# A fourth pair of split-weight buffers for two of the working tiles, and splits up to three chunks ahead

## The chip, the cores and the metric

The kernel runs on one NeuronCore of a Trainium2 chip. The metric is the device time of one execution in microseconds (us); several executions are timed and the median is given. A profile is one further execution, recorded by the hardware profiler.

## What is computed

Two layers of a hybrid diffusion backbone over 256 latent tokens and 256 context tokens, model width 1024, all in 32-bit floats:

```python
for l in range(DEPTH):                                  # DEPTH = 2
    # sh, sc, g: nine vectors per stream from the conditioning: s_c @ w_mod[l] + b_mod[l]
    x = x + 0.5 * g1 * swiglu(modulate(rms_norm(x, norm_g[l, 0]), sh1, sc1), ffn_w_in[l, 0], ffn_w_out[l, 0])
    h = h + 0.5 * cg1 * swiglu(...)                     # the context stream, same weights
    y, yc = token_mixer(modulate(rms_norm(x, ...)), modulate(rms_norm(h, ...)), ...)
    x = x + g2 * y
    x = x + 0.5 * g3 * swiglu(...)                      # second FFN; h too, in layer 0 only
```

`swiglu` has D_FF = 2816. The token mixer projects with one wide `w_in`, runs gated linear attention (4 heads), neighbourhood attention (16 heads) and grouped-query attention (8 heads), multiplies each result by a branch matrix, gates and adds them, and multiplies by `w_out`. The weights are read once from HBM, about 343 MB of traffic in all.

## The kernel before, in words

**Weights as a stream of chunks.** Every weight matrix is cut into chunks of 128 partitions x 1024 floats (512 KB), and `Program.chunk` (L281) puts them into one list in the order of use. A product in full precision is made of three matmuls (`mm3`, L494): weight and activation are each split into a part that TensorE's fast fp32r format holds exactly (`hi`) and the rest (`lo`), and hi·hi, hi·lo and lo·hi are added up in PSUM. So each chunk passes three places: a DMA on SyncE's queue (SP) loads it into a `w_raw` tile (L369), ScalarE (ACT) copies it, rounded, into `w_hi` (L382), and GpSimd (POOL) subtracts into `w_lo` (L385). TensorE (PE) then reads `w_hi` and `w_lo`.

**Buffers.** There are RAW_BUFS = 3 raw tiles and SPLIT_BUFS = 3 pairs of `w_hi` and `w_lo`. All other working tiles of the kernel (activations, attention weights, `mod_w` loads, temporaries of the norms) come from one pool `slot` of SLOTS = 54 tiles of 128 x 512 floats (`S`, L454).

**When a chunk is split.** The generator `splitter` (L373) runs through the chunks; its condition and the bookkeeping in `Program.run` (L355) are:

```python
for j, (src, a, b, do, halves) in enumerate(specs):
    while j > state["ci"] + SPLIT_AHEAD or (j >= SPLIT_BUFS and j - SPLIT_BUFS not in ended):
        yield None
    load(j + 1)
    ...
    load(j + 1 + RAW_BUFS)
...
fn(parts.pop(ci))
if ci + 1 not in self.kept:
    ended[ci] = self.clock.now
if ci in self.kept:
    ended[ci - 1] = self.clock.now
```

Here `ci` is the chunk whose matmuls are being issued. Chunk j is split once chunk j - SPLIT_BUFS has ended, and at most SPLIT_AHEAD chunks ahead. After the split of chunk j, chunk j + 3 is loaded into the raw tile that chunk j leaves.

**Pairs.** Most chunks are used one by one. Some are used two at a time: the first is kept (`kept`) and its matmuls are interleaved with those of the second, and neither has ended before both have. Two such pairs follow each other at the start of each FFN (`up` with `both`, L899: four chunks c0 to c3 for the two halves of the first block of the up-projection) and in `proj_f2` (L1085: queries and keys of the gated linear attention, twice per layer). The norm ahead of them delivers its result `u` tile by tile (`norm_chain`, L788; `need`, L831), in two halves r of 256 tokens, and the pairs let PE work on the first half while VectorE (DVE) makes the second. The last down-projection of an FFN and of `merge_out` (L1881) also end on a pair, so that the norm can start on one half.

**Order.** All instructions are issued in one order, decided while the program is built. A model clock (`Clock`, L54) estimates when each instruction would run; chunks are the main line, and at every `tick` (L351) a round is made: first the splitter, then pending norms and evacuations, then side jobs (attention heads, the conditioning vectors `mods`), each of which issues its next instruction once the model says that its inputs are there (`Gated`, L174). The model knows when the split buffers come free; it has no entry for the tiles of `slot`. Each engine then takes its own instructions strictly in this order, and waits on semaphores for the data and for the tiles it overwrites.

Of the kernel before, what the change touches and what calls it, by code (L numbers as in the profile page):

```python
# [36 lines left out]
C_GATE = 7712  # L37

RAW_BUFS = 3
SPLIT_BUFS = 3  # L40
SPLIT_AHEAD = 2
SLOTS = 54
LANES = 2
PE_MARGIN = 0.5
OTHER_SLACK = 0.1
# [155 lines left out]
class Program:  # L201
# [153 lines left out]
    def run(self):  # L355
# [17 lines left out]
        def splitter():  # L373
# [4 lines that stand above are left out]
                hi = self.wpool.tile([P, a, b], F32, name="w_hi", tag="w", padded_shape=[P, 1024 // b, b])  # L378
                lo = self.wpool.tile([P, a, b], F32, name="w_lo", tag="w", padded_shape=[P, 1024 // b, b])
                self.clock.floor[hi.name] = self.clock.floor[lo.name] = ended.get(j - SPLIT_BUFS, 0.0)  # L380
                raw = raws[j]
# [51 lines left out]
def tile_backbone(ctx: ExitStack, tc: tile.TileContext, I: dict, out: bass.AP):  # L433
# [4 lines left out]
    sml = ctx.enter_context(tc.tile_pool(name="sml", bufs=4))  # L438
    slot = ctx.enter_context(tc.tile_pool(name="slot", bufs=SLOTS))
    upool = ctx.enter_context(tc.tile_pool(name="upool", bufs=16))  # L440
    rpool = ctx.enter_context(tc.tile_pool(name="rpool", bufs=RAW_BUFS))
    wpool = ctx.enter_context(tc.tile_pool(name="wpool", bufs=2 * SPLIT_BUFS))
    psa = ctx.enter_context(tc.tile_pool(name="psa", bufs=4, space=PS))
# [1627 lines left out]
```

## Time and profile before

| | |
|---|---|
| median of 3 runs | 2881.67 us (2880.91 to 2881.89) |
| profiled execution | 2878.06 us |
| its span, first to last instruction | 2876.3 us |
| PE busy | 2777.6 us, 97% of the span |
| DVE, ACT, POOL busy | 58%, 35%, 45% of the span |
| DMA | 120 GB/s over the span |
| granted TensorE clock, mean | 0.985 |

The profile says for each engine how long it was busy. An idle stretch ends when the last thing that the engine waited for arrives, and the profile names that instruction ("idle before, <- releaser"). Time on the engine with hardly any idle stretches (PE here) is what the span consists of; its idle stretches and the stretches at the lower clock are what can be won. PEld is TensorE's loading of weights into the array, which overlaps the matmuls. POOL's times are rough. L196 and L169 are the helpers that issue all instructions, so instructions are told apart by the names of their tiles.

### The profile page before, as it was taken

Reading aid. Unit: us, or ns where it says so; the run is one execution under the profiler, and the core shown is the slowest. Engines: PE = TensorE matmul, PEld = TensorE weight load, DVE = VectorE, ACT = ScalarE, POOL = GpSimd, SP = SyncE. Lnnn points to the kernel's source line nnn. Section 1 sums busy time; section 2 is a strip of 40 time slices with the busy share of each in tenths; the row PEclk is TensorE's granted clock in tenths of the full one; section 3 lists DMA queues with packets and bytes.
Section 4 is the critical chain, followed back from the end, with each engine's and each line's share of the span. In section 5 each row is a group of like instructions: output and inputs, shape, how many; then the busy total and the mean of one; then the engine's idle time right before and its main releaser. Section 6 shows DMA issues by size and latency. Waiting matters only on the chain.

```text
span 2876.3 us, 39661 instructions
## 1 busy us (share of the span) xinstructions
PE 2777.6 (97%) x15547; PEld 2330.8 (81%) x15547; DVE 1662.6 (58%) x2970; ACT 1007.2 (35%) x1598; POOL 1288.1 (45%) x585
## 2 busy tenths in 40 slices
PE   8999998999999999999999989999999998999999
PEld 6888877778777888877888878888787777899899
DVE  5654566768765675675545575212555659757522
ACT  2222223433444344322312212222244345454443
POOL 3444433224333442434444434444433455657687
PEclk9999999999999999999999989999999999999999
DMA  6444443224222222433444434333323334435554
GB/s 228 159 147 133 151 129 107 77 81 131 80 73 78 81 74 62 161 125 109 144 143 139 161 102 146 101 96 99 110 70 85 95 100 115 132 103 180 172 184 155
DMA packets 295647, 346.46 MB, mean 120 GB/s; under 512 B 15541, under 2 KB 238806, under 8 KB 295460
## 3 DMA queue, kind: packets, MB, share of 16 engines
q1 hardware_dynamic: 294964, 343.58, 38.0%
q8 instruction: 122, 2.00, 0.3%
q14 instruction: 65, 0.53, 0.1%
q0 software_dynamic: 320, 0.28, 0.0%
q10 hardware_dynamic: 176, 0.07, 0.0%
HBM read 342.83 MB, written 1.05 MB: 120 GB/s over the span
## 4 chain that ended last, share of the span: by engine, by line
PE 86%; DVE 8%; issue 4%; POOL 1%; DMA 0%; ACT 0%; SPq 0%; DVEq 0%; POOLq 0%; ACTq 0%
PE up L169 28%; PE pf L169 17%; PE dn L169 15%; PE pt L169 15%; PE a_s L196 2%; PE a_t L196 2%; PE n_o L196 1%; POOL w_lo L196 1%; PE g_o L196 1%; PE q_o L196 1%; PE g_U L196 1%; PE a_qk L196 1%; DVE rs_a L196 1%; DVE z L169 1%; DVE a_p L196 1%
## 5 line engine op out<-in xcount | busy, mean ns | idle before, releaser
L196 POOL TENSOR_TENSOR w_lo<-w_raw,w_hi 128x1024 fp32r<-128x1024 f32 (+1 forms) x508 | 1228.2, 2422 | 1538.3 <-ACT w_hi L196 1480.3
L196 ACT CAST w_hi<-w_raw 128x1024 fp32r<-128x1024 f32 (+1 forms) x504 | 520.6, 1036 | 993.5 <-issue 311.9
L169 PE MATMUL up<-u_hi,w_lo 128*128 128x512 f32 (+1 forms) x1504 | 534.3, 355 | 16.1 <-POOL w_lo L196 16.0
L169 PE MATMUL up<-u_hi,w_hi 128*128 128x512 f32 (+1 forms) x1504 | 536.5, 357 | 6.4 <-DVE u_hi L196 4.1
L169 PE MATMUL up<-u_lo,w_hi 128*128 128x512 f32 (+1 forms) x1504 | 534.3, 355 | 5.0 <-DVE u_lo L196 4.8
L196 DVE SCALAR_TENSOR_TENSOR mod_acc<-mod_w,scv,mod_acc 128x512 f32<-128x512 f32 x364 | 372.7, 1070 | 57.3 <-DMA mod_w<-w_mod 57.0
L169 PE MATMUL dn<-ff_h,w_hi 128*128 128x512 f32 (+1 forms) x1528 | 396.8, 349 | 0.0
L169 PEld LDWEIGHTS up<-u_hi,w_hi 128*128 128x128 f32 x1504 | 290.9, 193 | 56.0 <-issue 11.0
L169 PEld LDWEIGHTS up<-u_hi,w_lo 128*128 128x128 f32 x1504 | 290.9, 193 | 54.9 <-POOL w_lo L196 17.1
L169 PEld LDWEIGHTS up<-u_lo,w_hi 128*128 128x128 f32 x1504 | 290.7, 193 | 43.4 <-DVE u_lo L196 6.0
L169 PEld LDWEIGHTS dn<-ff_h,w_hi 128*128 128x128 f32 x1528 | 267.6, 189 | 38.9 <-ACT w_hi L196 1.7
L169 PE MATMUL dn<-ff_h,w_lo 128*128 128x512 f32 (+1 forms) x764 | 265.9, 348 | 0.0
L169 PE MATMUL pt<-w_hi,u_hi 128*128 128x512 f32 x640 | 261.8, 409 | 0.0
L169 PE MATMUL pf<-u_hi,w_hi 128*128 128x256 f32 (+1 forms) x736 | 250.9, 341 | 10.3 <-DVE u_hi L196 7.0
L169 PE MATMUL pt<-w_hi,u_lo 128*128 128x512 f32 x640 | 250.8, 392 | 0.0
L169 PE MATMUL pt<-w_lo,u_hi 128*128 128x512 f32 x640 | 250.5, 391 | 0.0
L169 PE MATMUL pf<-u_hi,w_lo 128*128 128x256 f32 (+1 forms) x736 | 239.9, 326 | 8.7 <-POOL w_lo L196 8.7
L169 PE MATMUL pf<-u_lo,w_hi 128*128 128x256 f32 (+1 forms) x736 | 240.3, 327 | 5.8 <-DVE u_lo L196 5.7
L169 DVE TENSOR_TENSOR ff_h<-ff_a,up 128x512 f32<-128x512 f32 (+1 forms) x88 | 53.3, 620 | 317.0 <-PE up L169 278.7
L169 PE MATMUL pf<-y,w_hi 128*128 128x512 f32 (+1 forms) x768 | 195.6, 345 | 3.1 <-DVE y L196 1.9
L169 PEld LDWEIGHTS pf<-u_hi,w_hi 128*128 128x128 f32 x736 | 143.7, 195 | 30.9 <-issue 9.4
L169 DVE SCALAR_TENSOR_TENSOR x<-dn,ff_g,x 128x256 f32<-128x256 f32 x112 | 47.1, 478 | 202.0 <-PE dn L169 201.8
(227 smaller groups left out, 4043.0 us busy)
## 6 DMA issues: line engine op xcount, KB each, us to landing
w_raw<-ffn_w_in SPq DMA_DIRECT2D x176, 512.0 KB
w_raw<-w_in SPq DMA_DIRECT2D x168, 512.0 KB
mod_w<-w_mod SPq DMA_DIRECT2D x288, 256.0 KB
w_raw<-ffn_w_out SPq DMA_DIRECT2D x80, 512.0 KB
w_raw<-w_branch SPq DMA_DIRECT2D x48, 512.0 KB
w_raw<-w_out SPq DMA_DIRECT2D x16, 512.0 KB
w_raw<-ffn_w_out SPq DMA_DIRECT2D x16, 256.0 KB
n_rel<-nat_rpb SPq DMA_DIRECT2D x32, 109.5 KB
```

Source lines behind the costliest of these rows:

```text
L169: return real(*args, **kw)
L196: return real(*args, **kw)
```

## The change

```diff
 RAW_BUFS = 3
-SPLIT_BUFS = 3
-SPLIT_AHEAD = 2
-SLOTS = 54
+SPLIT_BUFS = 4
+SPLIT_AHEAD = 3
+SLOTS = 52
```

There are now four pairs `w_hi`, `w_lo`; chunk j is split once chunk j - 4 has ended, and up to three chunks ahead of the one in use. Two of the 54 working tiles go. Nothing else in the text differs; the order of instructions is worked out anew by the same rules.

## Rows read from the trace of the kernel before

**Rows 1.** The page: busy time of each engine and its share of the span.
```profile
PE 2777.6 (97%) x15547; PEld 2330.8 (81%) x15547; DVE 1662.6 (58%) x2970; ACT 1007.2 (35%) x1598; POOL 1288.1 (45%) x585
```

**Rows 2.** The waits of PE, whole span: for whom, us in total, times, longest.
```profile
PE up L169 <- POOL w_lo L196: 16.0, 4, 6.8
PE pf L169 <- POOL w_lo L196: 8.7, 3, 4.8
```

**Rows 3.** Timeline of PE, where it waits for a split: start, us, [idle before].
```profile
47.52 0.39 PE L169 MATMUL up<-u_hi,w_lo 128*128 128x256 f32 x1 [1.13 <-POOL w_lo L196]
...
438.59 0.58 PE L169 MATMUL pf<-u_hi,w_lo 128*128 128x256 f32 x1 [4.81 <-POOL w_lo L196]
...
497.10 0.39 PE L169 MATMUL pf<-u_hi,w_hi 128*128 128x256 f32 x1 [0.51 <-ACT w_hi L196]
499.54 0.39 PE L169 MATMUL pf<-u_hi,w_lo 128*128 128x256 f32 x1 [1.93 <-POOL w_lo L196]
...
1307.54 0.58 PE L169 MATMUL up<-u_hi,w_lo 128*128 128x256 f32 x1 [6.76 <-POOL w_lo L196]
...
1702.33 0.58 PE L169 MATMUL up<-u_hi,w_lo 128*128 128x256 f32 x1 [6.30 <-POOL w_lo L196]
...
2135.63 0.39 PE L169 MATMUL pf<-u_hi,w_hi 128*128 128x256 f32 x1 [1.02 <-ACT w_hi L196]
2138.12 0.39 PE L169 MATMUL pf<-u_hi,w_lo 128*128 128x256 f32 x1 [1.99 <-POOL w_lo L196]
...
2686.10 0.39 PE L169 MATMUL up<-u_hi,w_lo 128*128 128x256 f32 x1 [1.82 <-POOL w_lo L196]
```

**Rows 4.** Timelines of ACT and POOL where the second pair's split begins.
```profile
1299.06 2.00 ACT L196 CAST w_hi<-w_raw 128x1024 fp32r<-128x1024 f32 x2 [24.18 <-PE up L169]
...
1300.19 9.62 POOL L196 TENSOR_TENSOR w_lo<-w_raw,w_hi 128x1024 fp32r<-128x1024 f32 x2 [22.41 <-ACT w_hi L196]
```

**Rows 5.** Stretches after a stall (first: before one): us, busy by engine, PEclk, DMA.
```profile
430.00:433.50 3.50, 3.50 (x31) 3.50 (x30) 3.50 (x12) 1.44 (x2) 0.31 (x1) 1.00 0.00 0
...
438.59:443.00 4.41, 4.41 (x20) 4.41 (x21) 0.00 (x0) 0.00 (x0) 2.28 (x1) 0.50 0.64 153
...
1307.54:1313.50 5.96, 5.96 (x28) 5.96 (x29) 0.00 (x0) 0.00 (x0) 2.27 (x1) 0.50 0.73 224
...
1702.33:1706.10 3.77, 3.77 (x18) 3.77 (x19) 0.00 (x0) 0.00 (x0) 2.27 (x1) 0.51 0.51 155
...
499.50:504.00 4.50, 4.46 (x26) 4.47 (x27) 4.47 (x8) 0.46 (x1) 2.32 (x1) 0.68 0.61 150
2138.00:2143.00 5.00, 4.88 (x28) 4.88 (x29) 4.96 (x10) 0.00 (x0) 2.40 (x2) 0.66 0.64 175
```

**Rows 6.** Timeline of SP: loads of `w_raw`, the fourth chunk of two sites among them.
```profile
395.65 0.37 SPq L369 DMA_DIRECT2D w_raw<-w_in  x1
...
1261.30 0.38 SPq L369 DMA_DIRECT2D w_raw<-ffn_w_in  x1
```

**Rows 7.** Timeline of DVE: the last `u` tiles at two sites.
```profile
435.06 1.28 DVE L196 SCALAR_TENSOR_TENSOR u_lo<-n_t,mod,u_hi 128x256 fp32r<-128x256 f32 x3
...
1300.57 1.27 DVE L196 SCALAR_TENSOR_TENSOR u_lo<-n_t,mod,u_hi 128x256 fp32r<-128x256 f32 x3
```

**Rows 8.** Instructions on `w_lo` (ns, min/median/max), and ACT's waits for `w_hi`.
```profile
L196 POOL TENSOR_TENSOR w_lo<-w_raw,w_hi x508: 1258/2396/7294, 20.1 to 2865.7; 128x1024 fp32r<-128x1024 f32 x158, 128x512 fp32r<-128x512 f32 x12
...
ACT w_hi L196 <- PE up L169: 246.2, 63, 24.2
```

**Rows 9.** Timelines of POOL and DVE in the norm before the first pair.
```profile
406.89 5.14 POOL L196 TENSOR_TENSOR w_lo<-w_raw,w_hi 128x1024 fp32r<-128x1024 f32 x2 [11.26 <-ACT w_hi L196]
...
409.76 0.15 DVE L196 TENSOR_SCALAR rs_v<-n_ss 128x2 f32<-128x2 f32 x1
409.94 2.12 DVE L196 TENSOR_SCALAR rs_s<-rs_v 128x2 int32<-128x2 int32 x1
```

**Rows 10.** Groups of instructions, 930 to 1160 us: the last step of layer 0's grouped-query heads.
```profile
L196 ACT CAST y<-q_o 128x512 fp32r<-128x512 f32 x8 | 4.7, 586 | 15.3 <-PE q_o L196 15.3
```

## The prediction

> **What bounds the kernel now.** I read the page first. PE is busy for 2777.6 us, 97% of the span of 2876.3 us, so all that can be won on other engines lies in the 98.7 us in which PE is idle, and in stretches at the lower clock [rows 1]. POOL is busy for under half of the span, so splitting is not a rate limit; if it costs anything, it does so at single places. The waits of PE say so: waits for `w_lo` make 24.7 us, in only seven waits [rows 2]. Third, the timeline of PE, looked up for these waits: they lie at 47, 439, 500, 1308, 1702, 2138 and 2686 us, and two are preceded by a shorter wait for the `w_hi` of the same chunk [rows 3]. Each of the seven is the same place in the code: two pairs of chunks follow each other, and the second chunk of the second pair, c3, is missing. There are eight such places; at the eighth, in layer 1, PE waits for `u` instead. With three buffers c0, c1 and c2 fill them all, and c3 can be split only when PE has read c0 to the end, which in a pair is the end of the pair. The ACT row at 1299.06 shows it: ACT sits idle for 24.18 us and is released by the matmul of `up`, and only then are c3 and c4 split, 2.00 us on ACT and 9.62 us on POOL [rows 4]. PE has run through what c2 alone allows by 1300.8 and stands until 1307.54.
>
> Fourth, the stretches behind these waits. Just before a stall the granted clock is 1.00; behind the three long ones it is 0.50 for 4.4 to 6.0 us, and behind the two of about 2.4 us it is 0.68 and 0.66 over 4.5 and 5 us [rows 5]. So a stall is paid twice: once idle, once as matmuls at 1.2 instead of 2.4 GHz.
>
> **What the change does, part by part.**
>
> *Fourth pair of buffers, limit of three ahead (one edit in effect).* Chunk j now needs chunk j - 4, and c3's forerunner is the chunk before the pairs, which ends before PE reaches c0. So c3 is split in the norm ahead of the pairs, and c4 and c5, not c3 and c4, at the end of the first pair. The stalls removed are, in order [rows 3]: 1.13 + 4.81 + (0.51 + 1.93) + 6.76 + 6.30 + (1.02 + 1.99) + 1.82 = 26.3 us.
>
> The clock stretches behind them go too, since PE then runs through at 1.00. At clock k a stretch of t us does what takes k·t at full clock, so it costs (1 - k)·t: 4.41 x 0.50 + 5.96 x 0.50 + 3.77 x 0.49 + 4.50 x 0.32 + 5.00 x 0.34 = 2.2 + 3.0 + 1.8 + 1.4 + 1.7 = 10.1 us [rows 5]. Sum: 36.4 us. I assume that no other pause takes their place.
>
> What is late next at these places? First the raw chunk: c3's load is issued when c0's split ends, at 395.65 and 1261.30 us, 38 and 39 us ahead of the stalls at 433.8 and 1300.8 [rows 3, 6]. It is there. Second `u`: PE would reach the second half of tokens in the second pair 48 matmuls later, at 0.12 us (31 of them begin in the 3.50 us of the first of rows 5, and a few records are missing) 5.8 us after the present start of the stall. That is 439.6 and 1306.6, and the last `u_lo` ends at 436.3 and 1301.8 [rows 7]. It is there. Third c4: its split begins where c3's does now. The two splits from 1300.19 take until 1309.8, while PE needs c4 after the 96 matmuls of the second pair, at 1300.8 + 11.5 = 1312.3 [rows 4]. It is there, with 2.5 us to spare even for c5 behind it.
>
> *What is moved.* Each chunk's copy on ACT, subtraction on POOL and load on SP comes one chunk earlier in its queue; their number stays the same. ACT already waits at the head of its queue for PE to free a buffer, 246.2 us in 63 waits for `up` alone [rows 8]. That does not change: the splitter asks for chunk j when the end of j - 4 is near, where before it asked for j - 1 at the end of the same chunk. So the evacuations queued behind on ACT wait as now. The first use of the additional buffer adds one copy and one split (2.4 us of POOL at the median [rows 8]) ahead of time, covered by PE's matmuls; POOL's other instructions, the bias tables and small splits, come at most that later, and no wait of PE names them. On SP one more `w_raw` load, 0.37 us of issue [rows 6], passes `mod_w` loads once. Bounds for all of this, by the rows: from nothing to one split's 2.4 us at each of the eight places, 19 us; I take 1 us, since the number of splits in any stretch stays as it is.
>
> *Two working tiles fewer.* The trace shows no operation for this. Counted over the program, from each tile's first to its last access in issue order, at most 53 of the 54 are in use at once, in layer 0's attention heads, and under 49 in most of the rest. With 52 a tile there is overwritten soon after its last reader, and the writer may wait for that reader; the model clock does not see this. Below: nothing, if PE has always passed (it is busy for 97% of the span [rows 1], and most tiles' last readers are ones it has long run); a gain I exclude, since fewer buffers free nothing sooner. Above: a wait as long as one evacuation, 0.59 us [rows 10], for each of some 40 tiles in that stretch, 24 us. I take 2 us, near the lower end, since PE there has the projections' matmuls to run.
>
> **Sum**: 36.4 - 1 - 2 = 33.4 us off the profiled 2878.06 us: 2844.7. The median of the runs lies 3.6 us above the profiled run, so 2848 us.
>
> **Rivals.**
>
> *Splits meet the norm.* In the norm before the pairs POOL splits two chunks from 406.89 to 412.03, and a DVE instruction on two elements per partition takes 2.12 us in it, where the one ahead of it on the same two takes 0.15 [rows 9]. DVE's chain sets when PE may begin. If the new order puts one more split beside that chain, each of the five norms ahead of a pair or an FFN is up to 2.4 us longer [rows 8]: 5 x 2.4 = 12 us back, 2860 us; with part of the clock stretches kept (5 of 10.1 us), 2865. For it: the row. Against it: two splits come at the end of the previous stage with three buffers and also with four. The Trainium skill, "SBUF — State Buffer", section "Who interferes with whom", states that DVE and GpSimd share a port pair as an exclusive lock and that the one which issues second is blocked for the whole instruction. The DVE row agrees; POOL's longest split of 7.29 us [rows 8] shows that POOL pays as well. By that rule alone a split is worth delaying, not advancing, beside a norm.
>
> *The tiles bind.* Place: layer 0's heads, from some 990 to 1100 us. The eight grouped-query heads run one behind the other's tiles [rows 10]; PE takes its instructions in order, so a late transposed weight tile stops the projections too. It decides from 36.4 / 8 = 4.6 us per head on, and at 6 us per head the kernel ends at 2882 + 48 - 36 = 2894 us. For it: the count of 53. Against it: PE's own slack there is large, and I saw no wait on the release of a working tile worth a microsecond on PE.
>
> *The change does not do what it says.* If raw tiles, still three, or the gate of the model hold c3's split back to the pair's end, nothing moves: 2882 us. Against it: rows 6.
>
> **How the numbers follow.** The forecast, all stalls and clock stretches gone: 0.66, with its own range 2840 to 2858. Splits meeting the norm, or another partial loss: 0.14, 2858 to 2875. No effect: 0.07. Tiles bind: 0.13. The measurement tells some 0.2% from no change, 5.8 us; so faster means below 2876: 0.66 + 0.14 = 0.80; same 0.07; slower 0.13. The range for 8 in 10 takes in the first two cases: 2839 to 2875. Its lower end is the whole 36.4 us and a few more from the reordered second layer, where PE has other short pauses.
>
> **What would show it.** Right: in the waits of PE the `w_lo` total falls from 24.7 to below 3 us; PE's timeline runs through the second pairs near 433, 1295 and 1685 us; the granted clock there stays 1.00; ACT's copy of c3 lies ahead of the first pair. PE's idle time falls by some 26 us. Wrong: a wait of PE for `u_hi` or `u_lo` of similar length at the same places (the norm was the limit), waits of ACT or DVE on PE in layer 0's heads and PE idle between 990 and 1100 us (tiles), or the same seven waits.

## The result, and the profile after

The changed kernel takes 2865.39 us, median of 4 runs (2863.88 to 2867.4), the kernel before beside it 2881.29 us (2878.27 to 2881.89). The ratio is 0.9947, 95% interval 0.993 to 0.9965: faster by 16 us. The forecast was 2848 us, some 33 us faster. The time is inside the range, the sign is right, and over half of the gain is missing.

The profiled execution of the changed kernel is the longest of its four runs (2867.4 us), that of the kernel before (2878.06 us) is shorter than all four runs timed beside it, so the two traces differ by 10.7 us of span where the medians differ by 16.

The page after, busy time by engine, answers to [rows 1]:

```profile
PE 2776.0 (97%) x15547; PEld 2327.5 (81%) x15547; DVE 1687.5 (59%) x2969; ACT 1007.5 (35%) x1599; POOL 1291.4 (45%) x585
```

PE's idle time fell from 98.7 to 2865.6 - 2776.0 = 89.6 us: by 9 us, not 26. DVE is busy for 25 us more with as many instructions, so some of them take longer. The waits of PE after (for whom, us in total, times, longest) answer to [rows 2]:

```profile
PE a_t L196 <- DVE a_p L196: 9.6, 6, 6.2
PE g_oT L196 <- DVE g_o L196: 8.0, 3, 4.7
...
PE up L169 <- DVE u_hi L169: 4.6, 2, 2.3
...
PE pt L169 <- DVE g_k L169: 4.0, 1, 4.0
```

No wait for `w_lo` or `w_hi` is left in that view: the seven stalls are gone. What stands there instead are waits for DVE; the view of the kernel before has none for `g_o` or `g_k`. Three stretches behind the second pairs, where a stall stood before, show PE busy throughout and the clock at 0.92 to 1.00, where [rows 5] had 0.50 (the columns are those of [rows 5]):

```profile
442.00:450.00 8.00, 8.00 (x67) 7.91 (x67) 0.00 (x0) 1.39 (x3) 4.25 (x2) 1.00 0.55 162
...
1300.00:1316.00 16.00, 16.00 (x126) 16.00 (x126) 11.40 (x29) 3.28 (x3) 9.69 (x2) 0.92 0.07 20
1692.00:1706.00 14.00, 14.00 (x106) 13.43 (x105) 8.25 (x13) 4.55 (x7) 12.06 (x3) 1.00 0.31 95
```

**Where the gain went.** For the next table I added up PE's matmuls in each trace in the order of their starts, each at its columns' full-speed length, and compared the times at which two kernels have done the same work. The stretches are in us of the kernel before; each entry is what the kernel lost (+) or gained (-) in it; stretches in which the changed kernel moved by less than 1 us are left out. Where two stretches meet, up to 1 us can be put to either. The last column compares two kernels that the experiments below bring in.

```
stretch, what lies there        change  start_old  ahead2  pairs_only  hold3_after  hold3_before  before_q  before_p4 to after_p4
  35- 59  start, first pairs      +5.0    +1.5      +4.3     +2.7        +3.0          0.0         0.0       +2.1
 393- 449 norm, stall at 439      -6.3    -4.5      -7.7     -8.8        -8.7         -2.9        +3.5       -2.6
 449- 464 g_k                     +6.7    +5.7       0.0      0.0         0.0         +0.9         0.0       +2.6
 486- 529 stall at 500            -5.2    -5.2      -5.2     -5.2        -3.6         -1.5        +3.6       -3.8
 529- 989 layer 0, attention      +6.3    +6.3      +3.0     +3.0        +7.0         +7.6        +3.2       +4.0
1279-1389 stall at 1308           -9.5    -9.5      -9.9    -10.3        -9.3          0.0        -0.2       -6.8
1659-1789 stall at 1702          -10.6   -10.6     -12.8    -12.4       -10.1         -3.7        +0.3       -7.1
2044-2169 stall at 2138           -6.5    -6.5      -4.9     -6.5        -5.9         +1.4        -5.7       -4.5
2169-2339 layer 1, gated linear   +9.8    +9.8     +11.8     +9.2        +3.6         +1.9        +4.7       +5.0
2339-2659 layer 1, heads          +2.3    +2.0      -8.2     -8.1        -9.5         -7.7        -2.4        0.0
2659-2864 stall at 2686, end      -2.7    -2.6      -4.0     -0.1        -2.3         +9.8        +0.5       -4.0
whole span                       -10.7   -12.9     -33.4    -38.8       -36.1         +5.4        +7.3      -14.5
```

Column one: the six stretches with later stalls gain 6.3 + 5.2 + 9.5 + 10.6 + 6.5 + 2.7 = 40.8 us, more than the forecast's 36.4 for all seven. And 5.0 + 6.7 + 6.3 + 9.8 + 2.3 = 30.1 us are given back, where the forecast had 3.

**Three of these places in the trace.** First the start. Timelines after, of POOL, DVE and PE:

```profile
41.61 7.57 POOL L196 TENSOR_TENSOR w_lo<-w_raw,w_hi 128x512 fp32r<-128x512 f32 x4 [10.23 <-ACT w_hi L196]
...
41.65 2.96 DVE L169 SCALAR_TENSOR_TENSOR n_t<-x,n_A,rb 128x256 f32<-128x256 f32 x2
44.54 4.78 DVE L169 TENSOR_SCALAR u_hi<-n_t,mod 128x256 fp32r<-128x256 f32 x2
...
47.12 0.35 PE L169 MATMUL up<-u_hi,w_hi 128*128 128x256 f32 x1 [2.26 <-DVE u_hi L169]
49.77 0.45 PE L169 MATMUL up<-u_lo,w_hi 128*128 128x256 f32 x1 [2.30 <-DVE u_lo L169]
```

The same instructions of DVE in the kernel before, where POOL's split began only at 44.72:

```profile
42.04 0.88 DVE L169 SCALAR_TENSOR_TENSOR n_t<-x,n_A,rb 128x256 f32<-128x256 f32 x2
42.84 0.60 DVE L169 TENSOR_SCALAR u_hi<-n_t,mod 128x256 fp32r<-128x256 f32 x2
```

With the fourth pair c3 is split 3 us sooner (the first two of POOL's four, in halves), and c4 and c5 (the other two, whole) follow at once. All this falls into DVE's norm: beside c3 a pair of `n_t` takes 2.96 us in place of 0.88, beside c4 and c5 a pair of `u_hi` takes 4.78 in place of 0.60. Second, `g_k`. After, DVE and POOL, then PE's wait:

```profile
451.49 5.64 DVE L196 SCALAR_TENSOR_TENSOR mod_acc<-mod_w,scv,mod_acc 128x512 f32<-128x512 f32 x2
457.05 0.68 DVE L169 COPY g_k<-pf 128x512 f32<-128x512 f32 x1
...
451.20 5.38 POOL L196 TENSOR_TENSOR w_lo<-w_raw,w_hi 128x1024 fp32r<-128x1024 f32 x2 [4.95 <-ACT w_hi L196]
...
457.79 0.80 PE L169 MATMUL pt<-w_hi,u_hi 128*128 128x512 f32 x1 [4.02 <-DVE g_k L169]
```

Before, a pair of the same `mod_acc` instructions took 1.42 us, and `g_k` was copied at 451.41. Third, layer 1's gated linear attention, after:

```profile
2169.72 4.88 POOL L196 TENSOR_TENSOR w_lo<-w_raw,w_hi 128x1024 fp32r<-128x1024 f32 x2 [1.95 <-ACT w_hi L196]
2174.76 2.34 POOL L196 TENSOR_TENSOR w_lo<-w_raw,w_hi 128x1024 fp32r<-128x1024 f32 x1 [0.16 <-ACT w_hi L196]
...
2169.80 2.35 DVE L196 TENSOR_TENSOR rs_a<-rs_y 128x2 f32<-128x2 f32 x1
2172.19 0.16 DVE L196 TENSOR_TENSOR rs_a<-rs_a,rs_v 128x2 f32<-128x2 f32 x1
2172.38 2.24 DVE L196 SCALAR_TENSOR_TENSOR rs_y<-rs_a,rs_y 128x2 f32<-128x2 f32 x1
2174.65 0.16 DVE L196 TENSOR_TENSOR rs_a<-rs_y 128x2 f32<-128x2 f32 x1
2174.85 2.26 DVE L196 TENSOR_TENSOR rs_a<-rs_a,rs_v 128x2 f32<-128x2 f32 x1
...
2178.43 0.45 PE L196 MATMUL g_oT<-ident,g_o 128*128 128x128 f32 x1 [4.65 <-DVE g_o L196]
...
2178.00:2184.00 6.00, 5.57 (x17) 4.39 (x18) 1.74 (x4) 0.47 (x1) 0.00 (x0) 0.56 0.30 88
```

Three splits run one behind the other, and in each one DVE instruction on two elements stands for 2.2 to 2.4 us instead of 0.16. PE waits 4.65 us, and behind the wait the granted clock is 0.56 (the last line, a window with the columns of [rows 5]): the new stalls are paid twice, as the old ones were.

### The profile page after: what moved, and what is told of

Its sections match the earlier page's. It is cut to its first block, busy times and chain, and to the rows that moved or that the text cites. A ratio compares the mean times of both kernels' runs of the same rounds, so it can differ in the third digit from the quotient of the medians.

```text
span 2865.6 us, 39689 instructions
## 1 busy us (share of the span) xinstructions
PE 2776.0 (97%) x15547; PEld 2327.5 (81%) x15547; DVE 1687.5 (59%) x2969; ACT 1007.5 (35%) x1599; POOL 1291.4 (45%) x585
## 4 chain that ended last, share of the span: by engine, by line
PE 88%; DVE 10%; DMA 1%; issue 1%; ACT 0%; POOL 0%; SPq 0%; ACTq 0%; DVEq 0%
PE up L169 30%; PE pf L169 18%; PE dn L169 14%; PE pt L169 14%; PE a_s L196 2%; PE a_t L196 2%; PE n_o L196 1%; PE g_o L196 1%; DVE rs_a L196 1%; PE q_o L196 1%; PE g_U L196 1%; DVE rs_y L196 1%; DMA mod_w<-w_mod 1%; PE a_qk L196 1%; DVE a_p L196 1%
```

## The experiments

Each kernel was timed beside the kernel before, whose median was 2881.7 to 2883.6 us throughout.

**slots52: the two tiles alone**, in the kernel before.

```diff
-SLOTS = 54
+SLOTS = 52
```

> The kernel before with 52 working tiles in place of 54 and nothing else; the order of instructions is the same, since the model clock has no entry for these tiles. Theory 'moved splits' (what the change loses, it loses where a split or another instruction was moved, and the two tiles cost nothing): ratio to before 0.999 to 1.001, PE idle in layer 0's heads (1000 to 1290 us) as before. Rival 'the tiles bind': a part of the 17 us that are missing from the forecast is theirs: slower by 0.2 to 0.6%, 6 to 17 us, most of it between 990 and 1290 us.

2882.89 us, ratio 1.0003 (0.9993 to 1.0012). The two tiles cost nothing that can be measured in this order: by the interval between 2 us less and 3.5 us more. In the order of the changed kernel, the place of "The tiles bind" (layer 0's heads, 989 to 1279 us) moved by less than 1 us. So that rival falls.

**start_old: the first c3 as before**, in the changed kernel.

```diff
-... or (j >= SPLIT_BUFS and j - SPLIT_BUFS not in ended):
+... or (j >= SPLIT_BUFS and j - SPLIT_BUFS not in ended) or (j == 3 and 0 not in ended):
```

> The changed kernel, but the very first c3 (chunk 3) is split, as before the change, only when chunk 0 has ended; everything later as in the changed kernel. Theory 'a split beside the norm': the 5.0 us that the changed kernel loses from 35 to 50 us come back (the u_hi of DVE there take 0.6 us again, not 4.8), and the stall of 1.1 us at 47 us returns: 4 to 6 us faster than the changed kernel, about 2860. Rival 'absorbed': the start is waited for by a transfer or by the side jobs a little later, and the total moves by less than 1.5 us.

2857.95 us, ratio 0.9925 (0.9912 to 0.9938): 7 us below the changed kernel's median. In the traces the start loses 1.5 us in place of 5.0, and `u_hi` of that chain takes 0.61 us again; this profiled run is the longest of its five (2865.13 us), and its span is only 2.2 us shorter. The stall of 1.1 us did not return: on the device the edit did not delay c3, which is split from 40.38 us, 1.2 us sooner than in the changed kernel. It is done before DVE comes to that `n_t`. c4 and c5 meet only the next pair of `n_t`, and PE's one wait there is 2.6 us, for `mod_ev` behind it. So what the start loses hangs on which of DVE's instructions the splits meet, not on how early c3 is split.

**ahead2 and pairs_only: four pairs, used less.** The first keeps two chunks ahead; the second uses the fourth pair and the third chunk ahead for the seven later c3 alone.

```diff
-SPLIT_AHEAD = 3
+SPLIT_AHEAD = 2
```
```diff
-while j > state["ci"] + SPLIT_AHEAD or (j >= SPLIT_BUFS and j - SPLIT_BUFS not in ended):
+lim = SPLIT_BUFS if j > 3 and j in self.kept and j - 2 in self.kept else SPLIT_BUFS - 1
+while j > state["ci"] + lim - 1 or (j >= lim and j - lim not in ended):
```

> The changed kernel with its four pairs and 52 tiles, but splits at most two chunks ahead, as before the change. c3 is then split when the first pair starts, and not in the norm ahead of it. Theory 'moved splits': the waits of PE for w_lo stay below 5 us in all, since the first pair's 11 us of matmuls cover one split, and with the splits at their old distance elsewhere some of the 30 us given back stays: 2850 to 2862. Rival 'any re-planned order loses as much': the order is worked out anew here too, and the time is 2862 to 2870, like the changed kernel's. Rival 'the third chunk ahead is what removes the stalls': w_lo waits of 15 us or more return, 2870 or more.

> The changed kernel's four pairs and 52 tiles, but the fourth pair and the third chunk ahead are used for the seven later c3 alone (second chunk of a second pair, beyond the start); every other chunk keeps the old rule of three pairs and two ahead. Theory 'moved splits': the six later stalls and the clock stretches behind them go (some 34 us), and most of what the changed kernel gives back elsewhere stays: 2845 to 2855. Rival 'any re-planned order loses as much': what is gained at the sites is again given back in the mixers, 2860 to 2870.

2845.13 us, ratio 0.9871 (0.9858 to 0.9885), and 2839.06 us, ratio 0.9851 (0.9838 to 0.9865). Both lie below what the theory expected, and neither has a wait for `w_lo` left. So the fourth pair alone removes the stalls, and the third chunk ahead for every chunk costs 20 us on top. In the table, both kernels lose nothing at `g_k`, half as much in layer 0's attention, and gain 8 us in layer 1's heads; neither avoids the loss in layer 1's gated linear attention. The rival "any re-planned order loses as much" falls.

**hold3_after, hold3_before: does ACT's queue make the difference?** In the view of ACT's waits, those for a PE matmul ahead of a copy into `w_hi` add up to 639 us in 212 waits in the changed kernel, and to 230 us in 65 in ahead2. Here the split of a single chunk is held back by 3 us.

```diff
+if j >= SPLIT_BUFS and not {j, j + 1} & self.kept:
+    while not self.force and self.clock.now < ended[j - SPLIT_BUFS] + 3.0:
+        yield None
```

> The changed kernel, but a chunk outside the pairs is split no sooner than 3 us after its forerunner's end by the model clock. Theory 'ACT waits at the head of its queue': what two chunks ahead won over three (20 us with the same four buffers) is that ACT's copy no longer waits for PE to free the buffer (230 us in 65 waits for PE matmuls, against 639 in 212), and evacuations behind it come sooner. Then 3 us of hold do the same: these waits fall below 450 us and the time to 2845 to 2857. Rival 'only the order differs': the waits fall, the time stays at 2860 to 2870.

> The same hold of 3 us in the kernel before, with its three pairs, 54 tiles and two ahead. Theory 'ACT waits at the head of its queue': ACT's waits for PE at w_hi fall from 647 us to under 450, the seven stalls for w_lo stay as they are, and the kernel is 5 to 15 us faster than before, 2866 to 2876. Rival 'only the order differs': 2877 to 2890.

2842.93 us, ratio 0.9865 (0.9852 to 0.9879), with ACT's waits down to 346 us; and 2879.9 us, ratio 0.9999 (0.999 to 1.0008), with 380 us. The first came as expected, the second did not: with three pairs the hold makes splits late. PE's waits for `w_lo` in hold3_before:

```profile
PE up L169 <- POOL w_lo L196: 23.4, 15, 6.8
PE pf L169 <- POOL w_lo L196: 16.3, 10, 4.8
...
PE pt L169 <- POOL w_lo L196: 6.3, 6, 1.9
```

46.0 us in 31 waits, 21 us more than in [rows 2], so some 20 us must have been won elsewhere for the same total, 7.7 of them in layer 1's heads. The time lies in the range of the rival "only the order differs", but with these stalls it speaks neither for nor against the queue. The piece runs below do: there ACT waits longer than ever and the kernel is faster.

**before_q: how much an order moves by itself.**

```diff
-QUEUE = 1.0
+QUEUE = 1.2
```

> The kernel before with a neutral constant of the order changed: side jobs may be issued 1.2 us ahead of their engine by the model, not 1.0. No buffer differs, but on PE 6856 lines of the order do. It shows how far a re-planned order alone moves the time. Theory 'the losses have places' (a split or a wait at a named place): within 4 us of before, 2878 to 2886, the seven stalls the same. Rival 'any re-planned order is a lottery of tens of us': 2887 or more, or 2873 or less.

2885.96 us, ratio 1.0015 (1.0006 to 1.0024): 4 us, inside the range expected. The seven stalls did not stay the same, though: PE's waits for `w_lo` are 33.2 us in nine waits, the longest 8.3. In the table its places go up and down by 2 to 6 us each, layer 0's attention by +3.2. A loss of that size at one place needs no cause in the buffers.

**after_q4, after_p4: POOL's subtraction in pieces**, in the changed kernel. First four pieces that the planner knows of (two of 128x512 where a chunk has two rows):

```diff
-h = a // 2 if halves else a
+h = max(1, a // 4)
```

> The changed kernel, but POOL's subtraction of each chunk is issued in four pieces of 128x256 (two of 128x512 where the chunk has that shape) in place of one of 128x1024; the order is planned anew. Theory 'DVE stands while a split runs': in the changed kernel a DVE instruction on two elements takes 2.2 to 2.4 us, as long as the split beside it, three times in a row ahead of PE's 4.65 us wait for g_o. With pieces of some 0.6 us it stands for one piece at most: no such DVE instruction over 1 us, PE's waits for g_o fall from 8.0 to under 3 us, and the kernel is 5 to 15 us faster than the changed one, 2850 to 2860. Rival 'POOL pays': 1500 more instructions on POOL and as much blocking in sum; the same as the changed kernel or slower, 2863 to 2880.

2843.87 us, ratio 0.987 (0.9856 to 0.9883): 21 us below the changed kernel, more than expected. But two of the theory's signs failed: PE's waits for `g_o` fell from 8.0 only to 6.9 us, and the blocked instructions still take over 1 us. POOL and DVE there:

```profile
2151.34 7.51 POOL L196 TENSOR_TENSOR w_lo<-w_raw,w_hi 128x512 fp32r<-128x512 f32 x6 [1.80 <-ACT w_hi L196]
...
2151.41 1.23 DVE L196 TENSOR_TENSOR rs_a<-rs_y 128x2 f32<-128x2 f32 x1
2152.68 1.23 DVE L196 TENSOR_TENSOR rs_a<-rs_a,rs_v 128x2 f32<-128x2 f32 x1
```

Six such instructions of 1.2 us in place of three of 2.3. To part blocking from planning, the next kernel issues pieces that the planner doesn't know, so that the order stays the changed kernel's:

```diff
+class Parts:
+    def tensor_tensor(self, out, x, y, op):
+        n, b = out.shape[1], out.shape[2]
+        for i in range(n):
+            for s in range(0, b, 256):
+                part = (slice(None), slice(i, i + 1), slice(s, s + 256))
+                self.engine.tensor_tensor(out[part], x[part], y[part], op=op)
...
-yield from self.ggp.tensor_tensor(...)
+yield from self.gparts.tensor_tensor(...)      # Gated(prog, "POOL", Parts(nc.gpsimd))
```

> The changed kernel with its order of instructions kept, one for one: only POOL's subtraction of a chunk is issued as four instructions of 128x256, of which the planner knows nothing. It parts the two readings of the run with planned pieces, which gained 21 us. Theory 'pieces free DVE': DVE's instructions beside a split end sooner, the g_k copy near 457 us and the u_hi at the start come in time, 2843 to 2855. Rival 'the planner moved the splits' (each piece costs 0.1 us more in the model, so all splits and what is planned after them shift; where splits follow each other closely, each piece stops one more DVE instruction, and the sum is the same, as at g_o in the run with planned pieces: six instructions of 1.2 us in place of three of 2.3): 2860 to 2870.

2833.16 us, ratio 0.9838 (0.9825 to 0.9852): 32 us below the changed kernel, more than the theory expected, with the same order on PE. The page of after_p4:

```profile
PE 2764.4 (98%) x15547; PEld 2319.3 (82%) x15547; DVE 1516.1 (54%) x2969; ACT 1008.6 (36%) x1599; POOL 1637.3 (58%) x2061
```

DVE does the same 2969 instructions in 171 us less, and POOL pays with 346 us more, which it has. So a split does stop DVE, PE waits for that, and pieces relieve it. ACT's waits for PE matmuls ahead of `w_hi` went up, from 639 us to 738: the theory of ACT's queue falls as the main cause. At the three places shown, pieces give back 3.1, 4.1 and 6.0 us of 5.0, 6.7 and 9.8 (the same sum by work, changed kernel against after_p4).

**before_p4, pairs_p4: are the blocked chains the changed order's own?** The same class in the kernel before and in pairs_only.

> The kernel before, its order kept one for one, with POOL's subtraction issued in pieces of 128x256 as in the run 'after_p4'. Theory 'the blocked chains make up the shortfall' (in the changed order POOL's splits stop DVE at worse places than in the order before, and that is the 17 us missing from the forecast): the pieces gain far less here than the 32 us that they gained in the changed kernel, 10 to 20 us, 2862 to 2872; with pieces on both sides the change then gives 29 to 39 us, as forecast; the seven w_lo stalls stay. Rival 'pieces help every order alike': 26 to 38 us, 2844 to 2856, and the change gives some 17 us with pieces too, so the shortfall lies in the new order itself, not in DVE standing.

> The run 'pairs_only' (2839) with its order kept and POOL's subtraction in pieces of 128x256. Theory 'the blocked chains make up the shortfall': this order has fewer of them already, and the pieces gain less than in the changed kernel, 10 to 20 us: 2819 to 2829. Rival 'pieces help every order alike': 26 to 38 us, 2801 to 2813.

2846.99 us, ratio 0.987 (0.9854 to 0.9887), and 2818.42 us, ratio 0.977 (0.9755 to 0.9785). The pieces win 37 us in the kernel before, 32 in the changed one and 21 in pairs_only. With pieces on both sides the change gives 14 us, not 29 to 39. By what I had written, the rival has it in the first pair. By work, most of what the pieces win lies where the change did little: 18.2 us in the kernel before and 20.5 in the changed one come from layer 1's heads, where PE idles 18.8 and 20.7 us beside whole splits and some 6 beside pieces. So the 32 us are not a measure of what the change lost. And the expectation overlooked one thing: in pieces PE needn't wait for the whole of `w_lo`. Three of the stalls in before_p4, which answer to [rows 3]:

```profile
436.22 0.58 PE L169 MATMUL pf<-u_hi,w_lo 128*128 128x256 f32 x1 [3.18 <-POOL w_lo L212]
...
1299.48 0.58 PE L169 MATMUL up<-u_hi,w_lo 128*128 128x256 f32 x1 [5.21 <-POOL w_lo L212]
...
1690.56 0.58 PE L169 MATMUL up<-u_hi,w_lo 128*128 128x256 f32 x1 [4.86 <-POOL w_lo L212]
```

All seven places together fall from 26.3 to 16.3 us, so 10 us of the 37 are the very stalls that the change removes anyway. The table's last column has both effects: between the two kernels with pieces, the stalls' places give 2.6 + 3.8 + 6.8 + 7.1 + 4.5 + 4.0 = 28.8 us, and 2.1 + 2.6 + 4.0 + 5.0 = 13.7 us are given back, against 40.8 and 30.1 without pieces. At the start, `g_k` and the gated linear attention together 9.7 us remain of 21.5. Over half of the loss at these three places is thus DVE standing beside whole splits; the rest remains with short blocks, and stays in the order.

**best, best_q4, best_space: joining what won.** All have four pairs, two ahead as a rule, three for the seven later c3, and the first c3 waits for chunk 0; the second adds the planned pieces, the third keeps 4 us between splits.

```diff
+while j > state["ci"] + SPLIT_AHEAD + (j > 3 and j in self.kept and j - 2 in self.kept) or ... or (j == 3 and 0 not in ended):
...
+while not self.force and self.clock.now < last + 4.0:      # best_space only, single chunks
+    yield None
```

> Four pairs, 52 tiles, two chunks ahead as a rule; only the seven later c3 may be split three ahead, and the first c3 waits for chunk 0. It joins what won in the run with two ahead and in the run where the fourth pair serves the c3 alone. Theory 'places': the start's 4 us of the run with two ahead come back, the rest stays: 2837 to 2842. Rival 'each order has its own losses': 2843 to 2852.

> The kernel of the run 'best' with POOL's subtraction planned in pieces (four of 128x256, two of 128x512). Theory 'pieces free DVE': a further 5 to 15 us, 2825 to 2836. Rival 'the planner moved the splits': what the pieces gained with three ahead, the two ahead have gained already; 2836 to 2846.

> The kernel of the run 'best', but a chunk outside the pairs is split no sooner than 4 us, by the model, after the split before it, so that no three splits follow each other beside one chain of DVE. Theory 'bunched splits': the 7 to 8 us that the four-pair kernels lose between 2160 and 2300 us fall to 2 or 3, PE's wait for g_o of 4.6 us goes, and the kernel is 3 to 8 us faster than 'best'. Rival 'another chain is hit instead': within 3 us of 'best' or slower.

2842.79 us (ratio 0.9868, 0.9854 to 0.9881), 2822.52 us (0.9814, 0.9793 to 0.9835) and 2900.49 us (1.0071, 1.0058 to 1.0084). The first lies between the two ranges and does not beat pairs_only, which speaks for the rival. The pieces win some 20 us there too (the five runs spread from 2819 to 2835), more than I expected. The third is a clear miss, though PE's longest wait for `g_o` did fall from 4.7 to 1.8 us. PE's waits for `w_lo` in it:

```profile
PE pf L169 <- POOL w_lo L196: 26.1, 19, 2.3
PE up L169 <- POOL w_lo L196: 19.2, 18, 1.9
PE dn L169 <- POOL w_lo L196: 8.4, 5, 1.9
...
PE pt L169 <- POOL w_lo L196: 3.9, 2, 1.9
```

These are 44 waits for `w_lo`, 57.6 us, where the stalls before were seven. By work, the loss against the kernel before lies in layer 1's heads (+9.4 us) and behind them (+38.8): in the kernel before PE goes through the 67 chunks of the last 205 us at 3.1 us each, so with 4 us between splits it catches up with POOL. Such a hold must not be longer than PE's work on a chunk.

The fastest kernel is pairs_p4: 2818 us, 47 us below the changed kernel and 65 below the one before.

## Why the prediction was right or wrong

*Fourth pair of buffers.* Right. None of the seven stalls is left, c3 is split in the norm ahead of its pairs, its raw chunk and `u` were there, and the clock behind the second pairs stays at 0.92 to 1.00. The six later places gave 40.8 us, a little more than the forecast's 36.4. PE's idle time there fell by 27 us, 2 us more than the six stalls; the other 14 us are the same matmuls in less busy time, where 10.1 us were forecast for the clock. One reading was off without harm: behind the third long stall [rows 5] has 3.77 us at 0.51, not "4.4 to 6.0" at 0.50; the sum uses the right figures.

What the prediction did not ask is why the three long stalls were long. The late buffer is only a part of it. In the kernel before, c3's own split took 5.34, 7.29 and 6.83 us there, and 2.35 to 2.42 us at the three short ones after 490 us. POOL and DVE at the longest, with the last `u_lo` of [rows 7] between them:

```profile
1300.19 7.29 POOL L196 TENSOR_TENSOR w_lo<-w_raw,w_hi 128x1024 fp32r<-128x1024 f32 x1 [22.41 <-ACT w_hi L196]
...
1301.76 0.88 DVE L196 TENSOR_SCALAR mod_acc<-mod_w,scv 128x512 f32<-128x512 f32 x2
1302.55 2.74 DVE L196 SCALAR_TENSOR_TENSOR mod_acc<-mod_w,scv,mod_acc 128x512 f32<-128x512 f32 x4
```

DVE works without a gap until 1305.29, and the split ends 2.2 us later; at the other two long stalls it ends 2.1 and 2.2 us after DVE's row. Against a split of 2.4 us that is some 12 of the 26.3 us of stalls, an estimate from these rows. The change won these too, since it moved c3's split out of that row. c4 is split there now and takes 5.38, 7.36 and 7.91 us at the same three places, and PE does not wait for it.

*"I assume that no other pause takes their place."* This is the step that failed, with the 1 us under *What is moved* that goes with it. The time of 2865 us lies in the interval that the prediction gave 0.14 for a partial loss (2858 to 2875), not in the forecast's own 2840 to 2858; the stated range holds it only because it was drawn over both. New pauses took back 30.1 us: 5.0 at the start, 6.7 at `g_k`, 6.3 in layer 0's attention, 9.8 and 2.3 in layer 1. The step listed ACT's, POOL's and SP's queues past which a split is moved, and bounded the rest by one split on POOL at each of the eight places, where 25 of the 30 us arose away from them. It never asked which chain of DVE runs beside the moved split, though [rows 9] showed an instruction on two elements at 2.12 us. "Covered by PE's matmuls" was true of POOL and not of DVE.

*Splits meet the norm.* The rival had the mechanism and the wrong places. In the norm at 410 POOL still runs two splits, as before, as the rival's counterargument said; it is the first norm, the `mod_acc` ahead of `g_k` and the chain of layer 1's `g_o` that were hit. Its price of 12 us was too low: the start, `g_k` and layer 1's `g_o` alone lost 21.5, new waits and the clock behind them together. That its upper figure, 2865 us, is the time measured is luck: it added up other places, and old clock stretches that are gone. The Trainium skill ("SBUF — State Buffer", section "Who interferes with whom") states that a DVE instruction in a 2-port mode contends with GpSimd, and that the one which issues first holds the shared port pair for the whole instruction while the other is blocked. It says that a DVE instruction with two inputs in SBUF, such as the one on `rs_a` and `rs_v`, contends with a GpSimd instruction that reads SBUF. The trace agrees: that one's 2.26 us lies beside a split of 2.34 us, its 1.23 us beside pieces of half that length.

*Two working tiles fewer* cost nothing that slots52 could measure, where the forecast put 2 us, and "The tiles bind" falls with the same run.

*What remains open.* The 6.3 us in layer 0's attention are not explained by a wait: PE's largest two there are 1.6 and 0.9 us. Orders without the fourth pair lose there as well (3.2 us in before_q, 7.6 in hold3_before). And that two ahead beats three by 20 us is measured, but pieces take away only a part of it (pairs_p4 is 15 us ahead of after_p4, pairs_only 26 ahead of the changed kernel); I have no single cause for the remainder. By the table the 20 us lie in layer 1's heads (10.5 us), at `g_k` (6.7) and in layer 0's attention (3.3); in the heads hold3_before, with three pairs, wins 7.7 us as well.

## What to carry to other kernels

A buffer that lets work start sooner changes which other work it runs beside. Before a moved instruction is costed at nothing, look not only at the queue it goes into, but at every engine that it can stop while it runs, and there at chains of short instructions that PE waits for. And give additional depth to the places that need it: the fourth pair for seven chunks won 43 us, the same pair for every chunk 16.

## What the runs showed of the hardware

In layer 1's chain of dependent DVE instructions ahead of `g_o`, one stands for each of POOL's, however short these are: three of 2.3 us beside three splits, six of 1.2 us beside pieces of 128x512, nine of 0.65 to 0.68 us beside pieces of 128x256. Between two whole splits one more, of 0.16 us, passes. POOL and DVE in after_p4, where the chain stands nine times:

```profile
2155.82 8.43 POOL L212 TENSOR_TENSOR w_lo<-w_raw,w_hi 128x256 fp32r<-128x256 f32 x12 [1.53 <-ACT w_hi L196]
...
2155.89 0.68 DVE L196 TENSOR_TENSOR rs_a<-rs_y 128x2 f32<-128x2 f32 x1
...
2161.46 0.65 DVE L196 SCALAR_TENSOR_TENSOR rs_y<-rs_a,rs_y 128x2 f32<-128x2 f32 x1
...
2163.07 0.45 PE L196 MATMUL g_oT<-ident,g_o 128*128 128x128 f32 x1 [3.19 <-DVE g_o L196]
```

The sum is 6.9, 7.3 and 6.0 us. So pieces help little where many tiny instructions depend on each other (PE's wait only fell from 4.65 to 3.19 us), and much where few instructions stand ahead of something urgent: the pair of `mod_acc` ahead of `g_k` fell from 5.64 to 2.35 us.

POOL can stand for longer than one instruction of DVE. At the three long stalls it stood until a row of DVE's without a gap was over: in the kernel before, c3's split at 1300.19 ended 2.2 us after the row's end, and in before_p4 its first piece, a quarter of the work, ended 0.6 us after the end of the same row at 1298.85:

```profile
1293.78 5.65 POOL L212 TENSOR_TENSOR w_lo<-w_raw,w_hi 128x256 fp32r<-128x256 f32 x1 [20.17 <-ACT w_hi L196]
```

That is why pieces took only 4.6 us off the three long stalls. It is not so at every such row: at `g_k` in the changed kernel POOL's split began at 451.20, beside DVE's `mod_acc`, and there DVE stood. What decides it, no run here shows.
